# A decoder layer's MLP: first product by chunk pairs, w2's work in pieces, gate and residual at finished row blocks

## The chip, the cores and the metric

The kernel runs on one core of one Trainium2 chip. The metric is device time in microseconds (us) of one execution. The core has five engines with an instruction queue each: TensorE (PE, matmuls), VectorE (DVE), ScalarE (ACT), GpSimd (POOL) and SyncE (SP), which issues all DMA transfers between HBM and the on-chip memory (SBUF). Matmul results go to PSUM, which has eight banks of 128x512 float32. Each engine works its queue in order, and an instruction that waits holds up what stands behind it.

## The reference, cut to what matters

Sequence 2048, model width 1024, MLP width 4096, one layer, float32:

```python
    sh1, sc1, gt1, sh2, sc2, gt2 = split(silu(c) @ w_ada + b_ada)
    ...                                            # attention and retention give a and r
    y = concatenate([a, r]) @ w_out
    x = layer_norm(ALPHA * x + gt1 * y, ln1_g, ln1_b)
    h = x * (1.0 + sc2) + sh2
    f = square(relu(h @ w_ff1)) @ w_ff2
    x = layer_norm(ALPHA * x + gt2 * f, ln2_g, ln2_b)
```

The change lies in the last five lines.

## The kernel before, in words

**Products.** float32 precision is kept by splitting both operands of a product into a high and a low part: ACT copies to the high part (`split`, line 125), DVE or POOL subtracts to get the low part (line 128). `mm3` then runs three matmuls (lines 131 to 133), each 128x128 by 128x512. Both MLP products are tiled two by two, and each tile product is made with seven block products instead of eight (P1 to P7, added up in four accumulators X, Y, Z, W).

**The w_out stage** (lines 921 to 1010) goes over the 16 row blocks of 128 rows, last ones first. The weights are loaded in quarters, times the gate row gt1 (line 954), split, and kept in two pools: `wo0` for the left 512 columns, `wo1` for the right ones. Raw weights pass through `wor`, which has two buffers. For each row block, psY is the product; DVE adds the input residual (line 997) to get z; layer norm without gain follows on ACT. Then POOL makes x2 = z * (ALPHA ln1_g) + ALPHA ln1_b (lines 1003, 1004), and x2 goes to HBM (`ax2_d`): it is the residual of the last layer norm.

**The first MLP product** (`up`) goes over two halves of the rows (1024 each), and in a half over 16 chunks `c` of 256 MLP columns. A chunk has 84 matmuls of 512 columns: seven products of 12. The two w_ff1 tiles of a chunk are 512 KB loads (`w1r`), four in flight. Sums of weight blocks are made on POOL (DVE for the first four chunks, line 1074), then split into `w1h` and `w1l` (`w1p`, five buffers of each). `split_h` makes the seven h operands of a half (`hh`, `hl`), which stay until its end. Results are added on DVE out of PSUM, go through relu and square on ACT, and are stored to `g_d`. Chunks 0 and 1 run side by side, product by product; the others are written one after the other.

**w2's work** (`prep`) is done inside this stage, since the second product needs the same seven block combinations of w_ff2. A unit loads 1 MB (`w2r`, from the four `hraw` buffers), multiplies it by gt2 (line 1129, two DVE operations of 128x1024), and makes seven pieces: subtraction where needed, split into a tile `w2s`, store of 512 KB to `wt_d` (line 1137). `w2s` has two buffers, so a piece's split waits until the store of the piece two before it has landed. There are 16 units, eight in each half; `PREP` says after which chunk a unit is written down.

**The second MLP product** (`down`) goes over the two halves, and in a half over four steps `s` of 1024 MLP rows, seven products of 48 matmuls (each in two parts `q`). Its weights come back from `wt_d`, its activations `a4` from `g_d`. Results are added in SBUF (`acc`, one 128x1024 tile for a row block, line 1252). At s = 0 `acc` is loaded with the residual from `ax2_d` (`load_acc`), so all later work is addition. In the last step, P2 is taken ahead of P7 and P4: after it the first four row blocks of the half are complete, after P4 the other four. `finish` does the last layer norm: statistics on DVE (line 188), then either ACT, POOL times g2 (line 1199) and POOL or DVE plus b2 (line 1200), or, for t in FV4 of half 1, two `scalar_tensor_tensor` passes on DVE (lines 1191, 1194).

**What sets the order.** The program's text gives the dependencies; the order on each engine is laid out when the kernel is built, by a scheduler that goes by its own estimate of time (`schedule_with_timeline_sim`). Pools that are opened later may lie on the memory of pools that were closed; a tile then waits for what used the memory before. Instructions of text far apart may so stand next to each other in a queue.

## Time and profile before

| | us |
|---|---|
| median of three runs | 2646.72 (2644.70 to 2647.34) |
| the profiled execution: its time, its span | 2645.24, 2643.5 |
| last matmul of attention; first of w_out | 1080.23; 1082.26 |
| busy in the span: PE, DVE, ACT, POOL | 2457.8, 1809.5, 1188.1, 1126.6 |
| the last piece of w2 is issued | 1897.5 |

A row of the timeline gives start, length, engine, line, operation and operands (output <- inputs, with the partitions x elements of each), and in brackets how long the engine was idle before it and whom it waited for. PE's share is high everywhere, and since its matmuls overlap, a stretch is best judged by how many matmuls it holds: a stretch without losses has 443 in 100 us. The line numbers of the rows are those of the kernel before.

### The profile page before, as it was taken

What the parts mean: (1) busy time and instruction counts of PE and PEld (TensorE: products, weight loads), DVE (VectorE), ACT (ScalarE), POOL (GpSimd) and SP (SyncE); (2) the same over time, 40 slices, a digit from 0 to 9 for tenths busy, and PEclk for the clock granted to TensorE, in tenths of its full rate; (3) what the DMA queues carried; (4) which work ended last, traced back from release to release, by engine and by line L of the source; (5) the groups of instructions that cost most, each with busy time, mean ns of one, the idle gap of its engine ahead of it and who ended that gap; (6) DMA issues with size and microseconds to landing.
All of it is one profiled execution on the core that took longest, in us unless ns stands there. A gap on an engine that the chain in (4) does not pass through costs nothing.

```text
span 2643.5 us, 33756 instructions
## 1 busy us (share of the span) xinstructions
PE 2457.8 (93%) x11668; PEld 2028.1 (77%) x11668; DVE 1809.5 (68%) x2919; ACT 1188.1 (45%) x2317; POOL 1126.6 (43%) x1055
## 2 busy tenths in 40 slices
PE   6999999989999999899789999799999999999997
PEld 5887778877787878677577778677788888878885
DVE  8757675565767676766887755978645665776657
ACT  4653222246777777433455555455553111221111
POOL 4323545547978888577722223532220000330004
PEclk9999999988999999999889999899999999999998
DMA  9456341021112020655278863578838766776653
GB/s 327 146 196 224 108 133 50 31 73 32 48 37 61 20 62 13 219 183 192 104 263 268 280 229 107 174 255 278 293 123 349 271 245 256 295 301 244 225 191 127
DMA packets 194251, 464.69 MB, mean 176 GB/s; under 512 B 17560, under 2 KB 51736, under 8 KB 179744
## 3 DMA queue, kind: packets, MB, share of 16 engines
q1 hardware_dynamic: 194080, 462.54, 50.3%
q8 instruction: 92, 1.51, 0.2%
q14 instruction: 79, 0.65, 0.1%
HBM read 313.30 MB, written 149.17 MB: 175 GB/s over the span
## 4 chain that ended last, share of the span: by engine, by line
PE 54%; DVE 16%; DMA 13%; issue 6%; POOL 6%; ACT 5%; SPq 1%; DVEq 0%; ACTq 0%; POOLq 0%
DMA wt_d<-w2s 5%; PE d_W L131 4%; PE d_W L133 4%; PE d_W L132 4%; PE t L834 3%; DMA wad<-in_w_ada 2%; PE pj L133 2%; PE pj L132 2%; PE pj L131 2%; PE d_Z L132 2%; PE d_Z L133 2%; PE d_Z L131 2%; PE o L827 2%; PE o L825 2%; PE s L131 2%
## 5 line engine op out<-in xcount | busy, mean ns | idle before, releaser
L180 POOL TENSOR_SCALAR rs<-mv 128x1 f32<-128x1 f32 x32 | 16.0, 503 | 607.4 <-DVE mv L190 607.0
L128 DVE TENSOR_TENSOR w1l_P<-w,w1h_P 128x512 fp32r<-128x512 f32 x224 | 187.7, 844 | 69.4 <-ACT w1h_P L125 68.8
L806 ACT ACTIVATE p<-s,nm 128x512 f32<-128x512 f32 (+3 forms) x320 | 196.4, 627 | 41.8 <-DVE nm L803 38.3
L801 DVE TENSOR_REDUCE mx<-s 128x1 f32<-128x512 f32 (+3 forms) x288 | 175.0, 619 | 55.9 <-PE s L133 53.1
L1074 POOL TENSOR_TENSOR w<-w 128x512 f32<-128x512 f32 x56 | 81.7, 1463 | 286.7 <-DMA w<-in_w_ff 214.6
L125 ACT ACTIVATE w1h_P<-w 128x512 fp32r<-128x512 f32 x224 | 136.9, 622 | 108.2 <-PE u_Y L132 26.8
L850 POOL TENSOR_TENSOR tl<-tf,th 128x512 fp32r<-128x512 f32 x144 | 184.4, 1292 | 1.7
L834 PE MATMUL t<-ident,p 128*128 128x128 f32 x1088 | 164.3, 276 | 5.6 <-ACT tf L845 1.9
L834 PEld LDWEIGHTS t<-ident,p 128*128 128x128 f32 x1088 | 130.6, 142 | 30.8 <-ACT tf L845 6.1
L131 PE MATMUL pj<-wbh,hhb 128*128 128x512 f32 x384 | 151.3, 396 | 0.9 <-ACT wbh L125 0.5
L133 PE MATMUL pj<-wbh,hlb 128*128 128x512 f32 x384 | 152.1, 397 | 0.0
L132 PE MATMUL pj<-wbl,hhb 128*128 128x512 f32 x384 | 151.9, 396 | 0.2 <-DVE wbl L128 0.2
L131 PE MATMUL s<-kt,qt 96*128 96x512 f32 (+3 forms) x320 | 130.4, 408 | 11.5 <-ACT p L806 9.7
L1074 POOL TENSOR_TENSOR w<-w,w 128x512 f32<-128x512 f32 x56 | 81.8, 1461 | 133.8 <-DVE w1l_P L128 132.2
L128 DVE TENSOR_TENSOR w2s<-w2r,w2s 128x512 fp32r<-128x512 f32 x112 | 92.1, 825 | 66.8 <-ACT w2s L125 66.5
L125 ACT ACTIVATE w2s<-w2r 128x512 fp32r<-128x512 f32 x112 | 70.2, 628 | 146.0 <-DMA wt_d<-w2s 123.0
L827 PE MATMUL o<-tl,v 128*128 128x512 f32 (+2 forms) x320 | 123.3, 394 | 7.1 <-DVE tl L128 4.8
L825 PE MATMUL o<-th,v 128*128 128x512 f32 (+2 forms) x320 | 121.9, 385 | 5.6 <-DVE osum L861 4.5
L132 PE MATMUL s<-kt,qt 96*128 96x512 f32 (+3 forms) x320 | 120.4, 376 | 3.7 <-DVE kt L128 3.7
L133 PE MATMUL s<-kt,qt 96*128 96x512 f32 (+3 forms) x320 | 120.1, 376 | 0.0
L131 PE MATMUL u_W<-hh_P,w1h_P 128*128 128x512 f32 x256 | 102.6, 401 | 15.8 <-ACT hh_P L125 6.5
L133 PE MATMUL u_X<-hh_P,w1l_P 128*128 128x512 f32 x256 | 104.1, 408 | 12.4 <-DVE w1l_P L128 12.3
(372 smaller groups left out, 7850.6 us busy)
## 6 DMA issues: line engine op xcount, KB each, us to landing
wP<-wt_d SPq DMA_DIRECT2D x112, 1024.0 KB, 4.8
wt_d<-w2s SPq DMA_DIRECT2D x112, 512.0 KB, 4.9
w<-in_w_ff SPq DMA_DIRECT2D x64, 512.0 KB, 5.2
a<-g_d SPq DMA_DIRECT2D x32, 1024.0 KB, 6.3
g_d<-v SPq DMA_DIRECT2D x96, 256.0 KB, 4.2
wad<-in_w_ada SPq DMA_DIRECT2D x64, 256.0 KB, 2.9
w2r<-in_w_ff SPq DMA_DIRECT2D x16, 1024.0 KB, 7.7
x<-in_x SPq DMA_DIRECT2D x16, 512.0 KB, 8.2
```

The costliest lines, as they stand in the source:

```text
L125: A.activation(hi, x, AF.Copy)
L128: lo_eng.tensor_tensor(lo, x, hi.bitcast(F32), op=OP.subtract)
L131: T.matmul(ps, sh, mh, start=start, stop=False, skip_group_check=more)
L132: T.matmul(ps, sh, ml, start=False, stop=False, skip_group_check=more)
L133: T.matmul(ps, sl, mh, start=False, stop=stop, skip_group_check=more)
L801: V.tensor_reduce(mx[:, j:j + 1], ps[:, :n], op=OP.max, axis=AX.X)
L806: A.activation(pt[:, :m], b[:, :m], AF.Exp, bias=nm, accum_out=rs[:, qi, j:j + 1])
L825: T.matmul(po[:, cs], w, th[:, cs], start=(done == 0), stop=False)
L827: T.matmul(po[:, cs], w, tl[:, cs], start=False, stop=(done == nk))
L834: T.transpose(tp[:, qi * P:(qi + 1) * P], pts[h, 4 * qb + qi, kb // 4][1][:, kb % 4 * P:(kb % 4 + 1) * P], ident)
L850: (V if mode == "C" else G).tensor_tensor(tl[:, cs], tf[:, cs], th[:, cs].bitcast(F32), op=OP.subtract)
L1074: (V if half == 0 and c < W1V else G).tensor_tensor(src, *sub, op=op)
```

## The change

- **w_out stage.** The second multiplication row set (`ag1`, `ab1`) and x2 are gone; z itself is stored (`z_d`). The pools are opened in another order: `wo0` after `wo1`, `ax3` and `c3`.
- **First product.** All chunks run in pairs, product by product (P1 of both, P5 of both, ...), in the order P1, P5, P6, P7, P3, P4, P2. w_ff1 comes in quarters of 256 KB with two buffers for each quarter of each chunk of a pair. `split_h` hands out its seven operands one at a time, and those of half 1 are written into the last pair of half 0.
- **w2's work.** `prep` gives control back after every piece, and its 56 pieces of a half are written evenly between the products, from the seventh product step of the first pair on (a pair later in half 1). The multiplication by gt2 is gone.
- **Second product.** At s = 0 `acc` is no more loaded: the first addition to each quarter is an ACT copy out of PSUM. When a row block is complete, `residual` loads its z (two buffers, `ztp`) and makes x2 on POOL, and `gate` multiplies `acc` by gt2 and adds x2 on DVE. In the last product of half 1, gating is done ahead of the product, and the product's own results are gated one by one (tile y). `acc` of the first four row blocks has one buffer instead of two.
- **Buffers.** HSO and the pools of both products are opened in another order.

```diff
@@ w_out stage
     wor = pool(p3, "wor", 2)
-    wo0 = pool(p3, "wo0")
-    c3 = pool(p3, "c3")
     wo1 = pool(p3, "wo1")
     ax3 = pool(p3, "ax3", 2)
+    c3 = pool(p3, "c3")
+    wo0 = pool(p3, "wo0")
     x3 = pool(p3, "x3", 2)
-    c3b = pool(p3, "c3b")
...
-                    x2 = x3.tile([P, D], F32, tag="x2", name=f"x2_{tt}")
-                    G.tensor_tensor(x2, z, ag1, op=OP.mult)
-                    G.tensor_tensor(x2, x2, ab1, op=OP.add)
-                    Q.dma_start(ax2_d[tt], x2)
+                    Q.dma_start(z_d[tt], z)
@@ up, prep and their loop
-        for m in range(2):
-            t = w1r.tile([P, 2, 512], F32, tag="raw", name=f"w1_{half}_{c}_{m}")
-            Q.dma_start(t.rearrange("p j c -> p (j c)"), I["w_ff1"][2 * c + m].rearrange("p k c -> p (k c)"))
+        for m, j in ((0, 0), (1, 0), (1, 1), (0, 1)):
+            t = w1r.tile([P, 512], F32, tag=f"r{m}{j}", name=f"w1_{half}_{c}_{m}{j}")
+            Q.dma_start(t, I["w_ff1"][2 * c + m][:, 4 * j:4 * j + 4].rearrange("p k c -> p (k c)"))
...
-        for i in range(2):
-            V.tensor_tensor(b[:, i], b[:, i], gt2, op=OP.mult)
...
             Q.dma_start(wt_d[s][x][k // 2][:, :, k % 2], t.bitcast(F32))
+            yield
...
+        slots = [i for i in range(7 * NCH) if half or i < 7 * NCH - 8]
+        slots = slots[14:] if half else slots[12:]
+        nxt = split_h(1, Hn) if half == 0 else None
+        for c in range(0, NCH, 2):
+            pair = [up(half, x, H) for x in (c, c + 1)]
+            for x in range(7):
+                for y in range(2):
+                    next(pair[y], None)
+                    i = 7 * c + 2 * x + y
+                    if i in slots:
+                        while count < min(want, -(-(slots.index(i) + 1) * want // len(slots))):
+                            next(todo, None)
+                            count += 1
+                if nxt is not None and c == NCH - 2:
+                    next(nxt, None)
@@ second product
+    def residual(half, t):
+        zt = ztp.tile([P, D], F32, tag="zt", name=f"zt{half}_{t}")
+        with tc.issue_after(wdma[-1]):
+            Q.dma_start(zt, z_d[4 * border[2 * half + t // 4] + t % 4])
+        G.tensor_tensor(zt, zt, ag1, op=OP.mult)
+        G.tensor_tensor(zt, zt, ab1, op=OP.add)
+        return zt
+
+    def gate(f, zt):
+        V.tensor_tensor(f, f, gt2, op=OP.mult)
+        V.tensor_tensor(f, f, zt, op=OP.add)
+
     def finish(half, t):
         f = acc[t]
+        if half == 0 or t < 4:
+            gate(f, residual(half, t))
...
                 ops = [parts(q) for q in range(2)]
                 for tp in range(4):
+                    gate(acc[4 + tp], residual(half, 4 + tp))
+                for tp in range(4):
                     for k in range(4):
                         mm(tp, k, *ops[k // 2])
+                    y = ztp.tile([P, D], F32, tag="zt", name=f"y{tp}")[:, 0:512]
+                    V.tensor_tensor(y, ps[ch, tp], gt2[:, 0:512], op=OP.mult)
+                    V.tensor_tensor(acc[4 + tp][:, 0:512], acc[4 + tp][:, 0:512], y, op=OP.add)
+                return
...
-                        load_acc(half, 4 * i + tp)
+                        acc[4 * i + tp] = acs[4 * i + tp].tile([P, D], F32, tag="c", name=f"acc{half}_{4 * i + tp}")
                     c = acc[4 * i + tp][:, 512 * j:512 * j + 512]
-                    V.tensor_tensor(c, c, ps[ch, tp], op=OP.add)
+                    if s == 0 and name in ("P1", "P5", "P6", "P4"):
+                        A.activation(c, ps[ch, tp], AF.Copy)
+                    else:
+                        V.tensor_tensor(c, c, ps[ch, tp], op=OP.add)
```

How the change moves instructions is shown at three places. In a row stand line, operation, output <- inputs, and size; names carry the half and chunk (or step), and a running number that differs from build to build.

ACT in half 0 of the first product, before, from chunk 4's P7 on (w1h is a split of a w_ff1 block, w2s one of a w2 piece, u, v and r are results):

```order
L125 ACTIVATE w1h0_4_P7_15626<-w1_0_4_0_15565 128x512
L125 ACTIVATE w2s2_2_15726<-w2r2_15712 128x512
L1090 ACTIVATE v0_3_15555<-v0_3_15555 128x512
L125 ACTIVATE w1h0_4_P2_15643<-w1_0_4_0_15565 128x512
L1091 ACTIVATE v0_3_15555<-v0_3_15555 128x512
L125 ACTIVATE w1h0_4_P3_15662<-w1_0_4_1_15567 128x512
L1100 ACTIVATE u0_4_15622<-u0_4_X_15573 128x512
L125 ACTIVATE w2s2_3_15730<-w2r2_15712 128x512
L1090 ACTIVATE v0_3_15560<-v0_3_15560 128x512
L1091 ACTIVATE v0_3_15560<-v0_3_15560 128x512
L125 ACTIVATE w1h0_4_P4_15686<-w1_0_4_1_15567 128x512
L125 ACTIVATE w2s2_4_15734<-w2r2_15712 128x512
```

ACT in the same half after the change, at the pair of chunks 4 and 5:

```order
L126 ACTIVATE w1h0_4_P1_15508<-w1_0_4_00_15496 128x512
L126 ACTIVATE w2s2_6_15921<-w2r2_15682 128x512
L1090 ACTIVATE v0_3_15431<-v0_3_15431 128x512
L1091 ACTIVATE v0_3_15431<-v0_3_15431 128x512
L126 ACTIVATE w1h0_5_P1_15540<-w1_0_5_00_15528 128x512
L1090 ACTIVATE v0_2_15457<-v0_2_15457 128x512
L126 ACTIVATE w2s3_0_15964<-w2r3_15962 128x512
L1091 ACTIVATE v0_2_15457<-v0_2_15457 128x512
L126 ACTIVATE w1h0_4_P5_15557<-w1_0_4_10_15498 128x512
L126 ACTIVATE w2s3_1_16006<-w2r3_15962 128x512
L1090 ACTIVATE v0_3_15487<-v0_3_15487 128x512
L1091 ACTIVATE v0_3_15487<-v0_3_15487 128x512
```

In both, w2's pieces stand one at a time between the splits of the products. Over 14 products (two chunks), ACT's queue in half 0 has 3, 10, 11, 13, 12 and 7 pieces before, and 9, 10, 13, 12 and 12 now; in half 1 it has 4, 7, 12, 13, 13 and 7 before, and 8, 12, 13, 14 and 9 now.

DVE in the last step of half 0's second product, before, from the last addition of P2's result (X3) to the additions of P7's result (W0 and W1; gP4l is the low part of P4's operand, BN_STATS and BN_AGGR belong to the statistics):

```order
L1252 TENSOR_TENSOR acc0_3_20401<-acc0_3_20401,d0_3_X3_22047 128x512
L188 BN_STATS st_22140<-acc0_2_20398 128x6
L188 BN_STATS st_22154<-acc0_3_20401 128x6
L128 TENSOR_TENSOR gP4l0_3_0_22235<-a4_0_3_11_21766,gP4h0_3_0_22234 128x1024
...
L188 BN_STATS st_22154<-acc0_3_20401 128x6
...
L199 TENSOR_SCALAR nm_22132<-mv_22129,rs_22131 128x1
L128 TENSOR_TENSOR gP4l0_3_1_22265<-a4_0_3_11_21766,gP4h0_3_1_22264 128x1024
L199 TENSOR_SCALAR nm_22146<-mv_22143,rs_22145 128x1
L199 TENSOR_SCALAR nm_22160<-mv_22157,rs_22159 128x1
L1252 TENSOR_TENSOR acc0_4_20470<-acc0_4_20470,d0_3_W0_21772 128x512
L1252 TENSOR_TENSOR acc0_5_20473<-acc0_5_20473,d0_3_W1_21773 128x512
```

DVE there after the change:

```order
L1213 TENSOR_TENSOR acc0_1_20431<-acc0_1_20431,gt2_20352 128x1024
L1297 TENSOR_TENSOR acc0_3_20435<-acc0_3_20435,d0_3_X3_22083 128x512
L1213 TENSOR_TENSOR acc0_2_20433<-acc0_2_20433,gt2_20352 128x1024
L129 TENSOR_TENSOR gP4l0_3_0_22295<-a4_0_3_11_21802,gP4h0_3_0_22294 128x1024
L1214 TENSOR_TENSOR acc0_1_20431<-acc0_1_20431,zt0_1_22168 128x1024
L1213 TENSOR_TENSOR acc0_3_20435<-acc0_3_20435,gt2_20352 128x1024
L1214 TENSOR_TENSOR acc0_2_20433<-acc0_2_20433,zt0_2_22188 128x1024
L189 BN_STATS st_22174<-acc0_1_20431 128x6 x2
L129 TENSOR_TENSOR gP4l0_3_1_22325<-a4_0_3_11_21802,gP4h0_3_1_22324 128x1024
L189 BN_STATS st_22194<-acc0_2_20433 128x6 x2
L1297 TENSOR_TENSOR acc0_4_20503<-acc0_4_20503,d0_3_W0_21808 128x512
```

The multiplications by gt2 (L1213) and the additions of the residual (L1214, the residual tile is zt) now stand between P2's additions and the splits for P4 and ahead of P7's additions.

POOL in the tail, before, from the first row block that half 1 finishes (the sequence L180, L181 makes the reciprocal deviation, three rows of it left out):

```order
L1199 TENSOR_TENSOR acc1_0_22424<-acc1_0_22424,g2_20316 128x1024
L1200 TENSOR_TENSOR acc1_0_22424<-acc1_0_22424,b2_20317 128x1024
L180 TENSOR_SCALAR rs_24163<-mv_24161 128x1
...
L181 TENSOR_TENSOR rs4_24191<-rs4_24191,mhalf_115 128x1
L1199 TENSOR_TENSOR acc1_1_22427<-acc1_1_22427,g2_20316 128x1024
L1199 TENSOR_TENSOR acc1_2_22430<-acc1_2_22430,g2_20316 128x1024
L1200 TENSOR_TENSOR acc1_2_22430<-acc1_2_22430,b2_20317 128x1024
```

POOL in the tail after the change, from the second residual on:

```order
L1209 TENSOR_TENSOR zt1_1_24240<-zt1_1_24240,ab1_20354 128x1024
...
L1208 TENSOR_TENSOR zt1_2_24260<-zt1_2_24260,ag1_20353 128x1024
L1235 TENSOR_TENSOR acc1_0_22508<-acc1_0_22508,g2_20355 128x1024
L1209 TENSOR_TENSOR zt1_2_24260<-zt1_2_24260,ab1_20354 128x1024
L1236 TENSOR_TENSOR acc1_0_22508<-acc1_0_22508,b2_20356 128x1024
L1208 TENSOR_TENSOR zt1_3_24280<-zt1_3_24280,ag1_20353 128x1024
L1209 TENSOR_TENSOR zt1_3_24280<-zt1_3_24280,ab1_20354 128x1024
L1208 TENSOR_TENSOR zt1_4_24376<-zt1_4_24376,ag1_20353 128x1024
L181 TENSOR_SCALAR rs_24251<-mv_24249 128x1
L181 TENSOR_SCALAR rs_24271<-mv_24269 128x1
```

The tail's multiplications by g2 (now L1235) and additions of b2 (L1236) now alternate with the residual's two operations (L1208, L1209), which are done eight times in a half.

## Rows read from the trace of the kernel before

**Rows 1.** The page: busy us, share of the span, instructions, by engine.

```profile
PE 2457.8 (93%) x11668; PEld 2028.1 (77%) x11668; DVE 1809.5 (68%) x2919; ACT 1188.1 (45%) x2317; POOL 1126.6 (43%) x1055
```

**Rows 2.** Stretches: start:end us, length, busy us (instructions) by engine, granted clock, DMA share, GB/s.

```profile
1285.00:1345.00 60.00, 37.57 (x138) 29.12 (x138) 51.94 (x46) 26.68 (x34) 36.33 (x16) 0.72 0.37 133
1345.00:1561.00 216.00, 200.14 (x836) 159.81 (x835) 164.26 (x225) 119.87 (x214) 48.91 (x33) 0.97 0.83 274
1645.00:1705.00 60.00, 46.37 (x171) 35.47 (x170) 59.82 (x44) 28.08 (x43) 42.47 (x18) 0.86 0.42 136
1741.00:1897.00 156.00, 145.30 (x611) 115.44 (x611) 122.98 (x165) 92.57 (x165) 42.78 (x28) 0.98 0.80 270
...
2100.00:2200.00 100.00, 100.00 (x443) 82.82 (x442) 57.78 (x66) 20.17 (x19) 0.00 (x0) 1.00 0.69 251
2278.00:2344.00 66.00, 59.69 (x254) 48.33 (x253) 60.15 (x67) 19.98 (x18) 43.82 (x28) 0.97 0.84 320
2591.00:2643.50 52.50, 32.68 (x133) 26.20 (x131) 43.71 (x59) 8.17 (x7) 27.47 (x23) 0.84 0.29 112
```

**Rows 3.** Timeline, POOL, w_out weights times the gate: start, length, group, idle before.

```profile
1077.51 2.52 POOL L954 TENSOR_TENSOR wo<-wo,gt 128x512 f32<-128x512 f32 x2
1087.22 1.42 POOL L954 TENSOR_TENSOR wo<-wo,gt 128x512 f32<-128x512 f32 x1 [7.18 <-DMA wo<-in_w_out]
1091.47 1.87 POOL L954 TENSOR_TENSOR wo<-wo,gt 128x512 f32<-128x512 f32 x1 [2.83 <-DMA wo<-in_w_out]
```

**Rows 4.** Waits of PE, 1282 to 1345 us: who waited for whom, total, times, longest.

```profile
PE u_Y L132 <- DVE hl_P L128: 10.0, 2, 7.3
PE u_W L131 <- ACT hh_P L125: 6.5, 1, 6.5
PE u_Z L132 <- DVE hl_P L128: 3.8, 1, 3.8
```

**Rows 5.** Pieces of w2, half 0 (1330 to 1570): operations, then idle before them.

```profile
L125 ACT ACTIVATE w2s<-w2r x56: 614/632/635, 1334.7 to 1553.5; 128x512 fp32r<-128x512 f32 x56
L128 DVE TENSOR_TENSOR w2s<-w2r,w2s x56: 676/691/1815, 1336.3 to 1554.2; 128x512 fp32r<-128x512 f32 x56
L1137 SPq DMA_DIRECT2D wt_d<-w2s x56: 512/525/1177, 1337.0 to 1554.9; - x56
...
  DMA wt_d<-w2s: 68.8, 33
```

**Rows 6.** The same, half 1 (1685 to 1900 us).

```profile
L1137 SPq DMA_DIRECT2D wt_d<-w2s x56: 512/524/1293, 1691.7 to 1897.5; - x56
```

**Rows 7.** The page, DMA issues: count, KB each, median us to landing.

```profile
wt_d<-w2s SPq DMA_DIRECT2D x112, 512.0 KB, 4.9
...
w2r<-in_w_ff SPq DMA_DIRECT2D x16, 1024.0 KB, 7.7
```

**Rows 8.** The multiplications by gt2 in the pieces' way (line 1129).

```profile
L1129 DVE TENSOR_TENSOR w2r<-w2r,gt x32: 1211/1218/3423, 1333.4 to 1815.6; 128x1024 f32<-128x1024 f32 x32
```

**Rows 9.** Timeline of the tail: DVE and then POOL, at 2591 to 2614 us.

```profile
2591.20 0.69 DVE L1252 TENSOR_TENSOR acc<-acc,d_X 128x512 f32<-128x512 f32 x1 [0.47 <-PE d_X L133]
...
2608.51 5.50 DVE L1194 SCALAR_TENSOR_TENSOR acc<-acc,rs,b 128x512 f32<-128x512 f32 x2
...
2595.89 2.40 POOL L1199 TENSOR_TENSOR acc<-acc,g 128x1024 f32<-128x1024 f32 x1 [1.61 <-ACT acc L1198]
...
2607.70 5.75 POOL L1199 TENSOR_TENSOR acc<-acc,g 128x1024 f32<-128x1024 f32 x2
```

**Rows 10.** Groups in the tail, 2591 to 2643.5: count | busy, mean ns | idle before.

```profile
L1191 DVE SCALAR_TENSOR_TENSOR acc<-acc,mv,g 128x512 f32<-128x512 f32 x8 | 5.6, 744 | 0.0
...
L128 DVE TENSOR_TENSOR gP4l<-a,gP4h 128x1024 fp32r<-128x1024 f32 x2 | 2.4, 1210 | 0.0
```

**Rows 11.** Groups where half 0 ends and half 1 begins (2278 to 2345).

```profile
L1199 POOL TENSOR_TENSOR acc<-acc,g 128x1024 f32<-128x1024 f32 x8 | 22.8, 2866 | 5.0 <-ACT acc L1198 5.0
L1200 POOL TENSOR_TENSOR acc<-acc,b 128x1024 f32<-128x1024 f32 x4 | 13.2, 3310 | 0.2
```

120 lines of the change are left out of this document (64 added, 56 removed).

## The prediction

> **What bounds the kernel now.** I read the page first: PE is busy 93% of the span [rows 1], so a gain can only come from stretches where PE holds fewer matmuls than it could, and a loss from new such stretches. The table of stretches measures them. From 2100 to 2200 us PE issues 443 matmuls in 100 us at granted clock 1.00, 0.2257 us each; a stretch's loss is its length less its matmuls times that. By this, with [rows 2]: 60 - 138 x 0.2257 = 28.9 us are lost around the start of the first MLP product; 216 - 836 x 0.2257 = 27.3 where half 0 shares its time with w2's work; 60 - 171 x 0.2257 = 21.4 at the change of halves; 156 - 611 x 0.2257 = 18.1 with w2's work of half 1; 66 - 254 x 0.2257 = 8.7 where the second product changes halves. The tail runs from the addition of P2's result at 2591.20 [rows 9] to the end at 2643.5: 52.3 us, of which PE needs 133 x 0.2257 = 30. All that the change can win lies in the first four, about 96 us; what it adds lies in the last two.
>
> Two mechanisms decide. One is the **ring of two buffers** of w2's pieces: ACT was idle 68.8 us, 33 times, until a store had landed [rows 5], and the 56 pieces of a half leave every (1554.9 - 1337.0) / 55 = 3.96 us in half 0 and every (1897.5 - 1691.7) / 55 = 3.74 us in half 1 [rows 5, 6]. The other is that **DVE and POOL take turns** when both work from SBUF: two scalar_tensor_tensor halves of DVE, 0.74 us each by the mean of the undisturbed pass [rows 10], last 5.50 us beside two POOL multiplications, and these last 5.75 instead of twice the 2.40 of one alone [rows 9]. 1.5 + 4.8 = 6.3 is the time that both took together, from 2607.70 to 2608.51 + 5.50 = 2614.01. So I add DVE's operations with two SBUF inputs to POOL's, where both are queued; additions out of PSUM and statistics are left out of that sum.
>
> **The change, part by part.**
>
> *A. w_out's left weights.* Their last six quarters go through the two-buffer pool in three rounds, now at 1077.51, 1087.22 and 1091.47 [rows 3], so two of the three run while attention ends or psY has just begun. In the new order all three stand behind the right half's. The rounds are 4.25 us apart when nothing else is in the way and 9.7 at most. Three from 1091.47 end at 1104.3 to 1120.6; PE needs them after the 96 matmuls of the first two row blocks, 1082.26 + 96 x 0.2257 = 1103.9. Cost 0 to 17; I take **+9**, halfway. The 32 POOL operations of x2 that leave this stage are worth nothing by themselves; they count in B.
>
> *B. Start of the first product.* PE waits 10.0 + 6.5 + 3.8 = 20.3 us for the h operands [rows 4], because their work queues behind POOL's x2. In the new order four of the seven are split before psY ends, so these waits go. What is late next: on DVE the first subtraction of w2's first unit stands ahead of the first w1 split, and its 1 MB load takes 7.7 us [rows 7]. -20.3 + 7.7: **-13**, bounds -20 (the load is early) and -4.
>
> *C. w2's work.* The text now deals pieces evenly, but the scheduler had interleaved them before: the ACT rows of both kernels show one piece between two splits, and the counts for 14 products (10 to 13 before, 12 to 14 now) are higher now. Before, the pieces of half 0 lie between the 8th and 78th product in ACT's queue (70 products), now between the 4th and 67th (63); in half 1 it is 69 before and 60 now. A product is 12 x 0.2257 = 2.71 us, so PE would pass those places in 170.6 and 162.5 us. What it waits for is 55 times the ring's pace. The gt2 multiplications leave DVE's queue, 32 x 1.218 us [rows 8] over 112 pieces: 0.35 us each. So 3.61 and 3.39: 198.6 - 170.6 + 186.5 - 162.5 = 52 lost, against 27.3 + 18.1 = 45.4 now: **+7**. If the pace stays, 217.9 - 170.6 + 205.8 - 162.5 = 90.6: +45. If it falls below a product's 2.7 us, the whole 45 is won: -45. These are far apart; I take the value nearest the row, since 0.63 (ACT) + 0.69 (DVE) + 0.53 (SP) [rows 5] + 4.9 for landing [rows 7] is 6.75 for two pieces in flight, 3.4 a piece, with nothing between.
>
> The Trainium skill ("DMA: Bandwidth & Descriptors", "Anatomy of one DMA") fits 2.0 us plus the bytes over 436 GB/s for a DMA of another issuing path. For 512 KB that is an estimate of 3.2 us, so the ring could turn in 2.5 and C would be -45, the sum near 0. The landing row says 4.9 where the engines move some 270 GB/s, so the page's figure doesn't hold here.
>
> *D. Change of halves.* The seven operands of half 1 are the same operations, but given out through the last pair of half 0 and the first of half 1. The loss was 21.4; I take **-10**, half of it, since each operand still frees one of half 0's only after that half's last product that uses it; bounds -18 and 0.
>
> *E. The rest.* Twice as many w1 loads of half the size (64 more DMAs on SP), 16 loads of z for 16 of x2, five rows for all partitions in step 1 of half 0: hidden, unless a quarter's buffer is freed late. The 16 first additions become ACT copies, with ACT busy 20 of 66 us there [rows 2]. **+1**, 0 to +5.
>
> *F. Second product, change of halves.* Eight row blocks get two POOL operations and two DVE operations each (2.40 and 1.2 us, [rows 9, 10]) = 57.6 us of turn-taking. Before, POOL had 8 + 4 operations here [rows 11], which already last 2.87 and 3.31. In the new DVE queue 40 operations of 128x1024 with two SBUF inputs stand between P2's first addition and the last split for P7 of half 1's first step; POOL must do 20 by then (the first two residuals are earlier). 40 x 1.2 + 20 x 2.40 = 96 us. PE passes there in six and a half products, 6.5 x 48 x 0.2257 = 70.4. That is 25.6 lost if they pack without a gap, less the 8.7 lost already: +17. Above, nothing of the new work finds a gap: 57.6 less the four early POOL operations and the old loss, 57.6 - 9.6 - 8.7 = +39. I take **+24**, nearer to the lower end, since DVE and POOL still left gaps before (60.2 and 43.8 busy of 66 us, [rows 2]). Queued behind the gates on DVE are P7's additions, for which P4 waits, and P4's own splits.
>
> *G. Tail.* After P2's first addition, DVE has 16 gate operations, three splits and one addition of b2 (20 x 1.2 = 24), 16 scalar_tensor_tensor halves (11.8) and four additions of y (4 x 0.69 = 2.8): 38.6. POOL has 19 operations: 12 of residuals, 7 as before: 45.6. Together 84.2, against 52.3 for the whole tail now, of which the same kinds make 4.8 + 11.8 + 7 x 2.40 = 33.4. +32 if they pack, +45 with the present gaps (52.3 - 33.4 = 18.9) largely kept; **+34**. The residual's two buffers make this worse: each load waits for the gate of two blocks before.
>
> Sum: 9 - 13 + 7 - 10 + 1 + 24 + 34 = **+52**. The profiled execution took 2645.24, so 2697; it lies 1.5 below the median of the runs shown, so I say **2698**.
>
> **Rivals.**
> 1. *The first product recovers.* The ring keeps up (C -45), start and change of halves give their best (B -20, D -18, A 0, E 0), F and G as above: -83 + 58 = -25, 2620. For it: the gt2 multiplications gone, pairs give each split twice the time. Against: landing takes 4.9 us whatever the order. It decides below 2.7 us a piece. Chance 0.20.
> 2. *Residual and gate are hidden.* POOL is idle from 2100 to 2200 and DVE 42% [rows 2]; if z's loads and POOL's work came early, F would be 0 and G about +4, the sum -2: 2643. Against: two buffers, and the order that puts the rest behind P2's end. Chance 0.11.
> 3. *The ring keeps its old pace.* Then packing pieces into fewer products costs +45 in C, the sum is +90: 2735. Decided by whether the gt2 rows were in the ring's way at all. Chance 0.13.
>
> **How the numbers follow.** The forecast has 0.56. The range is 2632 to 2738: low enough for rival 2 and the better half of C's bounds, high enough for rival 3; most of rival 1 (0.14) and 0.06 above are left out. 0.2%, about 5 us, is what can be told from no change here. Faster: 0.20 + 0.06 of rival 2 = 0.26; same: 0.04 of rival 2 + 0.02 = 0.06; slower: 0.68.
>
> **What would show it.** After the change, pieces should leave every 3.4 to 3.6 us in both halves, with ACT still idle for landing stores; PE should show a loss of some 30 us after the last P2 of half 0's second product, with DVE rows of 128x1024 at 2 to 3.5 us beside POOL's; the tail from P2's first addition should last some 86 us. Wrong are: A, if psY's third row block starts before 1108; C, if PE shows no waits for w1h or w1l between the first pair and the last piece; F and G, if POOL's residual operations run before P2's end.

## The result, and the profile after the change

The changed kernel took 2690.65 us (median; 2689.74 to 2691.44), the kernel before 2645.71 (2642.19 to 2647.34) beside it: a ratio of 1.0172, 95% interval 1.0154 to 1.0189. The profiled execution has a span of 2689.6 us, 46.1 more than before. The direction, the size (2698 foretold) and the mechanism of the two terms that carry it (F and G) were right. A, the first product (B, C, D) and E missed by -6.8, -9.2 and +7.1 us, G by +7.5 and F by +0.6, and attention, which no term names, came out 5.0 shorter: these misses largely cancel, to -5.8 in sum, and that is luck.

The page of the kernel after, busy us by engine, to be held against [rows 1]: PE, DVE and POOL have as much work as before (PE has the same 11668 matmuls), in a longer span. What changed is where the work lies.

```profile
PE 2447.0 (91%) x11668; PEld 2028.9 (75%) x11668; DVE 1815.3 (67%) x2891; ACT 1209.6 (45%) x2349; POOL 1148.1 (43%) x1055
```

Cutting the span at events that both traces have gives the stages, in us. They run up to: the last matmul of attention; the last psY; the middle and the last matmul of the first product; the first of the second product ("gap"); DVE's first addition of P2's result in half 0's last step (this stretch is "second product, half 0", below also "down 0"); PE's first P2 matmul in half 1's first step ("change"); DVE's first addition of P2's result in half 1's last step; the end of the span ("tail").

| | before | after | difference | foretold |
|---|---|---|---|---|
| up to attention's end | 1080.2 | 1075.2 | -5.0 | |
| w_out | 208.2 | 210.4 | +2.2 | A +9 |
| first product, half 0 | 371.5 | 354.0 | -17.5 | B, C, D together |
| first product, half 1 | 342.0 | 334.3 | -7.7 | -16 |
| gap | 0.7 | 8.8 | +8.1 | E +1 |
| second product, half 0 | 275.1 | 276.8 | +1.7 | F +24, |
| change | 92.9 | 115.8 | +22.9 | these two |
| half 1 | 220.5 | 220.5 | 0 | |
| tail | 52.3 | 93.8 | +41.5 | G +34 |

The first product's half 0 is counted from the last psY on, so it holds the 16.0 us up to the first u matmul (1.0 before).

The table of stretches after the change, with the columns of [rows 2]:

```profile
1285.00:1345.00 60.00, 40.03 (x173) 32.12 (x172) 51.53 (x65) 36.14 (x53) 22.38 (x11) 0.83 0.70 242
1295.00:1510.00 215.00, 193.99 (x821) 156.07 (x821) 171.85 (x228) 128.17 (x220) 53.32 (x32) 0.95 0.85 290
1639.00:1836.00 197.00, 180.53 (x761) 147.18 (x760) 161.69 (x196) 116.93 (x206) 65.81 (x40) 0.96 0.82 281
2278.00:2362.00 84.00, 62.32 (x233) 48.08 (x232) 79.52 (x70) 24.61 (x29) 68.22 (x34) 0.88 0.54 198
2595.80:2689.60 93.80, 32.93 (x133) 26.35 (x131) 85.25 (x81) 7.99 (x7) 63.32 (x35) 0.67 0.26 96
```

The first row now loses 60 - 173 x 0.2257 = 21.0 us (28.9 before). The fourth, where the second product changes halves, loses 84 - 233 x 0.2257 = 31.4 (8.7 before), and DVE is busy for 79.5 of its 84 us. In the tail, DVE is busy 85.3 of 93.8 us and PE does the same 133 matmuls as before.

Why, the timeline of the tail shows (start, length, group), DVE first, then POOL:

```profile
2609.13 3.42 DVE L129 TENSOR_TENSOR gP4l<-a,gP4h 128x1024 fp32r<-128x1024 f32 x1
2612.47 3.42 DVE L1214 TENSOR_TENSOR acc<-acc,zt 128x1024 f32<-128x1024 f32 x1
2615.82 1.21 DVE L1213 TENSOR_TENSOR acc<-acc,gt 128x1024 f32<-128x1024 f32 x1
...
2620.41 1.27 DVE L189 BATCH_NORM_STATS2 st<-acc 128x6 f32<-128x512 f32 x2
2621.61 0.66 DVE L1297 TENSOR_TENSOR acc<-acc,d_W 128x512 f32<-128x512 f32 x1
...
2604.75 3.37 POOL L1235 TENSOR_TENSOR acc<-acc,g 128x1024 f32<-128x1024 f32 x1
2608.08 3.38 POOL L1209 TENSOR_TENSOR zt<-zt,ab 128x1024 f32<-128x1024 f32 x1
2611.43 3.38 POOL L1236 TENSOR_TENSOR acc<-acc,b 128x1024 f32<-128x1024 f32 x1
2620.36 2.35 POOL L1208 TENSOR_TENSOR zt<-zt,ag 128x1024 f32<-128x1024 f32 x1 [5.54 <-DMA zt<-z_d]
```

POOL's row that starts at 2608.08 ends at 2611.46; DVE's split, at hand since 2609.13, ends at 2612.55, 1.1 us later, about what it takes alone (1.21). POOL's next row then ends at 2614.81, 2.3 us after that, and DVE's next at 2615.89, again 1.1 later: strict turns, each waiting for the whole of the other. At 2620 DVE takes statistics and adds out of PSUM beside POOL, and neither is held (2.35 and 1.27). The Trainium skill ("SBUF — State Buffer", "SBUF: two separate sides") says just this: a DVE operation with two SBUF inputs and a POOL operation that reads SBUF share a pair of ports, which whichever starts first holds for its whole instruction. The trace agrees: an operation of 1.21 us lasts 3.42 beside one of 2.40.

### The profile page after: what moved, and what is told of

Read it like the earlier page. It is cut to its first block, busy times and chain, and to the rows that moved or that the text cites. A ratio compares the mean times of both kernels' runs of the same rounds, so it can differ in the third digit from the quotient of the medians.

```text
span 2689.6 us, 33970 instructions
## 1 busy us (share of the span) xinstructions
PE 2447.0 (91%) x11668; PEld 2028.9 (75%) x11668; DVE 1815.3 (67%) x2891; ACT 1209.6 (45%) x2349; POOL 1148.1 (43%) x1055
## 4 chain that ended last, share of the span: by engine, by line
PE 62%; DVE 16%; DMA 10%; issue 5%; ACT 4%; POOL 2%; SPq 0%; DVEq 0%; ACTq 0%; POOLq 0%
DMA wt_d<-w2s 4%; PE d_W L132 4%; PE d_W L133 4%; PE d_W L134 4%; PE t L835 3%; DMA wad<-in_w_ada 2%; PE o L826 2%; PE o L828 2%; PE d_Z L134 2%; PE d_Z L133 2%; PE pj L134 2%; PE d_Z L132 2%; PE pj L132 2%; PE pj L133 2%; PE s L132 2%
## 5 line engine op out<-in xcount | busy, mean ns | idle before, releaser
L1076 POOL TENSOR_TENSOR w<-w,w 128x512 f32<-128x512 f32 x112 | 167.7, 1503 | 377.7 <-DVE w1l_P L129 234.2
L129 DVE TENSOR_TENSOR w1l_P<-w,w1h_P 128x512 fp32r<-128x512 f32 x224 | 194.6, 872 | 65.7 <-ACT w1h_P L126 64.4
L807 ACT ACTIVATE p<-s,nm 128x512 f32<-128x512 f32 (+3 forms) x320 | 196.6, 627 | 39.7 <-DVE nm L804 36.2
L1208 POOL TENSOR_TENSOR zt<-zt,ag 128x1024 f32<-128x1024 f32 x16 | 44.1, 2762 | 355.6 <-DMA zt<-z_d 355.6
L126 ACT ACTIVATE w1h_P<-w 128x512 fp32r<-128x512 f32 x224 | 138.1, 622 | 97.4 <-PE u_Y L133 25.2
L129 DVE TENSOR_TENSOR w2s<-w2r,w2s 128x512 fp32r<-128x512 f32 x112 | 98.0, 876 | 57.7 <-ACT w2s L126 57.2
L132 PE MATMUL u_Z<-hh_P,w1h_P 128*128 128x512 f32 x256 | 104.9, 410 | 28.4 <-DVE v L1105 28.4
L132 PE MATMUL psY<-wo_h,mh 128*128 128x512 f32 x256 | 101.1, 400 | 10.8 <-ACT wo_h L126 10.3
L129 DVE TENSOR_TENSOR tl<-t,th 128x512 fp32r<-128x512 f32 (+3 forms) x176 | 92.7, 539 | 26.9 <-ACT th L126 25.7
```

Of the source, the lines that this page charges most:

```text
L126: A.activation(hi, x, AF.Copy)
L129: lo_eng.tensor_tensor(lo, x, hi.bitcast(F32), op=OP.subtract)
L132: T.matmul(ps, sh, mh, start=start, stop=False, skip_group_check=more)
L807: A.activation(pt[:, :m], b[:, :m], AF.Exp, bias=nm, accum_out=rs[:, qi, j:j + 1])
L1076: (V if half == 0 and c < W1V else G).tensor_tensor(src, *sub, op=op)
```

## The experiments

The ratios are against the kernel before, timed beside each. The stages of all profiled executions, in us (names as above; "up 0" and "up 1" are the halves of the first product):

| run | w_out | up 0 | up 1 | gap | down 0 | change | half 1 | tail | span |
|---|---|---|---|---|---|---|---|---|---|
| before | 208.2 | 371.5 | 342.0 | 0.7 | 275.1 | 92.9 | 220.5 | 52.3 | 2643.5 |
| after | 210.4 | 354.0 | 334.3 | 8.8 | 276.8 | 115.8 | 220.5 | 93.8 | 2689.6 |
| x2_early | 224.0 | 360.6 | 333.1 | 16.1 | 276.9 | 99.3 | 220.5 | 73.2 | 2673.0 |
| res_dve | 209.8 | 350.0 | 330.8 | 8.6 | 276.9 | 103.0 | 220.5 | 83.1 | 2658.1 |
| ztp4 | 210.5 | 353.3 | 331.7 | 8.4 | 278.3 | 115.8 | 220.5 | 89.1 | 2681.8 |
| gt2_prep | 210.5 | 356.7 | 339.5 | 8.7 | 283.9 | 109.3 | 220.5 | 76.9 | 2683.3 |
| up_only | 207.5 | 373.4 | 344.3 | 17.2 | 277.8 | 94.5 | 220.5 | 51.5 | 2661.8 |
| old_up | 209.1 | 359.3 | 339.7 | 11.7 | 277.2 | 112.4 | 220.5 | 94.0 | 2698.3 |
| wo0_first | 196.6 | 362.2 | 331.0 | 8.8 | 276.8 | 112.0 | 220.5 | 93.8 | 2677.6 |
| mid | 210.3 | 359.0 | 338.7 | 8.7 | 296.6 | 87.2 | 234.0 | 51.5 | 2659.8 |
| mid_old | 211.2 | 363.5 | 340.9 | 12.1 | 290.3 | 87.1 | 234.1 | 51.5 | 2663.6 |
| spread | 210.6 | 358.1 | 342.0 | 8.8 | 281.0 | 87.2 | 220.5 | 52.1 | 2634.5 |
| spread_wl | 210.8 | 360.0 | 338.1 | 2.2 | 281.9 | 87.2 | 220.5 | 52.4 | 2631.5 |
| spread_all | 196.4 | 361.6 | 340.1 | 2.8 | 283.2 | 87.2 | 220.5 | 51.5 | 2620.5 |

One caution: res_dve and ztp4 have the first product's text unchanged, and it takes 680.8 and 685.0 us in them against 688.3 after the change. The order is laid out anew in every build, so a difference below some 8 us in the first product can't be put down to an edit.

### What the finishing stretches cost

**res_dve**: the residual's two operations on DVE instead of POOL.

```diff
-        G.tensor_tensor(zt, zt, ag1, op=OP.mult)
-        G.tensor_tensor(zt, zt, ab1, op=OP.add)
+        V.tensor_tensor(zt, zt, ag1, op=OP.mult)
+        V.tensor_tensor(zt, zt, ab1, op=OP.add)
```

> The changed kernel with the residual's two operations on DVE instead of POOL, nothing else. Theory 1 (turn-taking): a POOL operation of 2.40 us is replaced by one of 1.2 in the same shared time, so the tail's sum falls from 84 to 84 - 12 x 1.2 = 70 and the tail from 93.8 to about 80; the change of halves gains about 10; 2660 to 2675. Rival (DVE is the bound by itself, POOL's work was free): 16 more DVE operations in each half cost 14 us in the tail and 10 to 14 at the change of halves, 2700 or more.

Measured 2662.94 us (2659.87 to 2664.32), ratio 1.0073 (1.0052 to 1.0094): 28 us faster than the change, by giving DVE, the busier of the two engines, 32 more operations. The finishing stretches make 23.5 of it (tail -10.7, change of halves -12.8, as foretold); the first product's -7.5 is no more than a new order moves. Groups of its tail, from 2590 us on (count | busy, mean ns):

```profile
L1214 DVE TENSOR_TENSOR acc<-acc,zt 128x1024 f32<-128x1024 f32 x7 | 12.5, 1801 | 0.0
...
L1208 DVE TENSOR_TENSOR zt<-zt,ag 128x1024 f32<-128x1024 f32 x5 | 5.9, 1203 | 0.6 <-DMA zt<-z_d 0.6
```

An operation that holds the ports for 2.40 us on POOL holds them for 1.20 on DVE. Had the two engines worked side by side, this edit would have made it slower. That turns are taken is shown.

**x2_early**: x2 is made in the w_out stage again and stored, the gate stays at the end.

```diff
+                    G.tensor_tensor(x2, z, xg1, op=OP.mult)
+                    G.tensor_tensor(x2, x2, xb1, op=OP.add)
-                    Q.dma_start(z_d[tt], z)
+                    Q.dma_start(z_d[tt], x2)
...
     def residual(half, t):
-        G.tensor_tensor(zt, zt, ag1, op=OP.mult)
-        G.tensor_tensor(zt, zt, ab1, op=OP.add)
```

> The changed kernel, but x2 is made by POOL in the w_out stage again and loaded ready; the gate on DVE stays. 24 POOL operations of 128x1024 leave the two finishing stretches, 32 come back in w_out. Theory 1 (turn-taking): the tail from P2's first addition has 38.6 + 7 x 2.40 = 55 us of turn-taking instead of 84, so 93.8 falls to some 70 to 75; the other change of halves loses some 12 instead of 33; up to 10 come back at the start of the first product. 2650 to 2665. Rival (the finishing stretches are long because a gate stands in DVE's queue ahead of other work, POOL doesn't matter): tail within 8 us of 93.8, 2680 or more.

Measured 2678.91 us (2673.69 to 2683.89), ratio 1.0135 (1.0108 to 1.0162), just short of the rival's 2680, yet the tail fell to 73.2 as the theory had it. Against the change, tail and change of halves give back 20.6 + 16.5 = 37 us, w_out takes 13.6, and the first product 5.4, which is within what a new order moves. The gap takes 7.3, in which PE waits for the second product's first weights (15.7 us of the 16.1). So x2's removal from the early stages was worth some 14 to 19 us there, and its new place cost 37; the total lies 14 us above the expected range, since more came back early than the 10 us allowed for, and the gap grew.

**gt2_prep**: gt2 is multiplied into w2 again; `gate` only adds the residual.

```diff
+        for i in range(2):
+            V.tensor_tensor(b[:, i], b[:, i], gt2, op=OP.mult)
...
-        V.tensor_tensor(f, f, gt2, op=OP.mult)
         V.tensor_tensor(f, f, zt, op=OP.add)
```

> The changed kernel with gt2 multiplied into w2 again, and no multiplication in the gate (the residual stays where the change puts it; three and one result buffers instead of four and two for gt2's memory). Theory 1 (a ring of w2 pieces that DVE's queue slows, and turn-taking at the finishing stretches): the second half of the first product takes some 10 us more (344 instead of 334), the tail 10 to 15 less, the change of halves 8 to 12 less: 2672 to 2684. Rival (gt2's multiplications cost the same wherever they stand, 1.2 us each on DVE): 2688 to 2694.

Measured 2685.27 us (2679.89 to 2688.84), ratio 1.0149 (1.0131 to 1.0168), between the two expectations. The stages tell more: tail -16.9, change -6.5, against down 0 +7.1 and the first product +7.9. The last is no larger than what a new order alone moves. What gt2 costs the ring of w2's pieces can be read, though, from the stores of the two halves (times in ns, then first and last start):

```profile
L1140 SPq DMA_DIRECT2D wt_d<-w2s x56: 512/519/613, 1311.3 to 1525.9; - x56
...
L1140 SPq DMA_DIRECT2D wt_d<-w2s x56: 512/519/798, 1656.8 to 1855.0; - x56
```

Pieces leave every 3.90 and 3.60 us, where the change, without gt2, has 3.64 and 3.41; stores land alike (4.0 and 3.9 us by the pages). So gt2's rows were in the ring's way, by 0.26 and 0.19 us a piece where the prediction took 0.35. The ring is 25 us longer in sum, the first product only 7.9: in half 0 PE passes 70 products beside the pieces, not 65.

**ztp4**: four buffers for the residual instead of two, paid for with one of the five weight buffers.

```diff
-WLB = 5
+WLB = 4
-    ztp = pool(p4b, "ztp", 2)
+    ztp = pool(p4b, "ztp", 4)
```

> The changed kernel with four buffers for z instead of two (and four instead of five for w2's weights, to make room). Theory 1 (turn-taking sets the finishing stretches): four more POOL operations come ahead of P2's end in each half, 4 x 2.40 = 9.6 us less in each: 2670 to 2682. Rival (the two buffers set them: every load of z waits for a gate two row blocks before): the tail falls by 20 us or more and the change of halves as well, 2650 or less.

Measured 2687.21 us (2683.57 to 2688.09), ratio 1.0164 (1.0142 to 1.0185), above what either expected. The tail is 4.7 shorter, the change of halves is not: this missed the turn-taking expectation too, which took four POOL operations out of each finishing stretch. In the tail the waits for z's loads go, but DVE's multiplications by gt2 then take 2458 ns (group of its tail) where they took 2158:

```profile
L1213 DVE TENSOR_TENSOR acc<-acc,gt 128x1024 f32<-128x1024 f32 x8 | 19.4, 2458 | 0.0
```

What POOL no longer waits for, it takes from DVE. The two buffers were a small part of the tail; what the weight buffer given up for them costs, no run tells.

### What the first product and the start are worth

**up_only**: the kernel before, with the change's first product and pieces (gt2 still in w2, x2 still in w_out, second product as before).

```diff
-        for c in range(NCH):
...
-            if c in PREP[half]:
-                prep(8 * half + PREP[half].index(c))
+        for c in range(0, NCH, 2):
+            pair = [up(half, x, H) for x in (c, c + 1)]
+            for x in range(7):
+                for y in range(2):
+                    next(pair[y], None)
...
-HSO = 6, 5, 4, "u", "w", 0, 1, 2, 3
+HSO = 6, 4, "u", 5, 3, 2, "s", "o", 0, 1, "w"
```

> The kernel before with the first product alone as changed (pairs, w_ff1 in quarters, w2's work in pieces, its pool order); w_out, x2, the multiplication by gt2 in w2's work and the second product are as before. One and three result buffers instead of two and four, since gt2 takes their memory. Theory 1 (turn-taking of DVE and POOL in the second product costs all of the loss, the first product gains): 2620 to 2641, from 2645.7 by the gains read at the start, half 0 and the change of halves (8 to 26 us). Rival (the pairs cost as much as they bring, since P3 now waits for DVE's addition out of Z): 2646 or more.

Measured 2662.27 us (2660.86 to 2664.15), ratio 1.0071 (1.0046 to 1.0096): the rival. With x2 and gt2 left in place, pairs and evenly dealt pieces gain nothing in the first product (717.7 us against 713.5), and the gap ahead of the second is 17.2: in its wait list there PE waits for the first weights alone.

```profile
PE d_W L132 <- DMA wP<-wt_d: 16.9, 1, 16.9
```

**old_up**: the reverse, the change with the first product, its loads and its buffers as before (w2 without gt2).

```diff
-        for c in range(0, NCH, 2):
-            pair = [up(half, x, H) for x in (c, c + 1)]
+        for c in range(NCH):
...
+            if c in PREP[half]:
+                prep(8 * half + PREP[half].index(c))
...
-        for m, j in ((0, 0), (1, 0), (1, 1), (0, 1)):
+        for m in range(2):
```

> The changed kernel with the first product and w2's work written as before (chunks one after the other, units whole, w_ff1 in 512 KB, the old pool order there), but without the multiplication by gt2; w_out, z, residual and gate stay changed. Theory 1 (pairs and pieces bring nothing by themselves; the first product got shorter because x2 left its start and gt2 left DVE's queue): 2680 to 2700, with the first product within 10 us of the changed kernel's. Rival (pairs and pieces make the gain): the first product is 20 us longer or more, 2708 or above.

Measured 2703.67 us (2700.11 to 2708.91), ratio 1.0227 (1.0208 to 1.0246), between theory and rival. Its first product takes 699.0 us against 688.3 after the change and 713.5 before: without x2 and gt2 the old form already gains 14.5, and pairs add some 11, little above what order alone moves.

**wo0_first**: the change with w_out's pools opened in the order of before.

```diff
+    wo0 = pool(p3, "wo0")
+    c3 = pool(p3, "c3")
     wo1 = pool(p3, "wo1")
     ax3 = pool(p3, "ax3", 2)
-    c3 = pool(p3, "c3")
-    wo0 = pool(p3, "wo0")
```

> The changed kernel with the pools of w_out in the order of the kernel before (wo0 ahead of wo1), nothing else. Theory of the prediction's part A: psY starts about 7 us earlier after attention, and PE has no waits of 10.3 and 8.7 us for wo_h and wo_l; 9 us less in all, 2676 to 2685. Rival (the late start is given back inside the stage, since the later row blocks then find z and the axl operands ready): within 4 us of 2690.

Measured 2680.46 us (2677.39 to 2684.68), ratio 1.0139 (1.0112 to 1.0165): as the theory of A has it. In the change, three rounds of POOL's multiplications by the gate start well into the stage (timeline of the kernel after, POOL), and PE waits for the split weights (its wait list, w_out):

```profile
1094.99 3.31 POOL L954 TENSOR_TENSOR wo<-wo,gt 128x512 f32<-128x512 f32 x2 [3.52 <-DVE axl L987]
1105.90 2.56 POOL L954 TENSOR_TENSOR wo<-wo,gt 128x512 f32<-128x512 f32 x2 [7.61 <-DMA wo<-in_w_out]
1111.79 2.55 POOL L954 TENSOR_TENSOR wo<-wo,gt 128x512 f32<-128x512 f32 x2 [3.33 <-DMA wo<-in_w_out]
```

```profile
PE psY L132 <- ACT wo_h L126: 10.3, 2, 8.7
PE psY L133 <- DVE wo_l L129: 8.7, 2, 6.6
```

With the old order the last round is at 1088.77, these waits shrink to 0.6 us, and the stage takes 196.6. That is 11.6 less than before the change, with x2's operations gone. The first product is 4.9 longer than after the change, which order alone could do. Counted up to the first u matmul, it is 209.6 us from attention's end, against 226.4 after the change and 209.3 before: in both changed kernels PE waits for the last row blocks' z ahead of the first u.

### Where residual and gate could go instead

**mid**: gt2 in w2, and all eight residuals of a half added together after its step s = 1; nothing is left for the finishing stretches.

```diff
+            if s == 1:
+                for t in range(8):
+                    V.tensor_tensor(acc[t], acc[t], residual(half, t), op=OP.add)
...
-            gate(f, residual(half, t))
```

> The changed kernel with gt2 multiplied into w2 again, and with the residual made by POOL and added by DVE after the second of the four steps of each half, where POOL is idle, instead of where row blocks are finished; acc still begins with an ACT copy. Theory 1 (the loss is turn-taking at the finishing stretches alone): both finishing stretches as long as in the kernel before (tail 52, the step after the change of halves 70), the first product 10 longer than in the changed kernel: 2632 to 2645. Rival (32 POOL and 16 DVE operations more in the second product cost their time wherever they are): 2660 or more.

Measured 2662.04 us (2660.51 to 2664.67), ratio 1.0064 (1.0049 to 1.0079): the rival. Tail and change of halves are back, even better than before, but the place of the eight residuals now loses 20 and 13.5 us. PE's wait list there, and DVE's timeline at half 0:

```profile
PE d_Z L132 <- DVE acc L1290: 9.3, 1, 9.3
```

```profile
2139.14 3.36 DVE L1325 TENSOR_TENSOR acc<-acc,zt 128x1024 f32<-128x1024 f32 x1
...
2144.76 1.21 DVE L129 TENSOR_TENSOR gP1l<-a,gP1h 128x1024 fp32r<-128x1024 f32 x1
...
2148.17 3.40 DVE L129 TENSOR_TENSOR gP1l<-a,gP1h 128x1024 fp32r<-128x1024 f32 x1
```

Even in a stretch where POOL had been idle, 16 POOL operations in a lump make a DVE split take 3.40 us instead of 1.21, and PE waits for DVE. Rival 2's hiding place exists, but not for all at once.

**mid_old**: the same with the first product as before (the diff of old_up).

> The same as the last kernel, with the first product and w2's work as before the change (gt2 in the same place). Theory 1 (pairs and pieces bring nothing; the end of the first product got 8 to 16 us worse by the other order of the pools): 2625 to 2640, not above the kernel with pairs. Rival (pairs and pieces shorten the first product): 12 us or more above the kernel with pairs.

Measured 2665.65 us (2663.65 to 2668.87), ratio 1.0078 (1.0063 to 1.0093). This missed the expectation twice: by mid's own loss in the middle steps, and because it lies 3.6 above mid and not below. Its first product takes 704.4 against 697.7; 6.7 us is within what order alone moves, so with gt2 in w2's work pairs are worth a few us at most.

**spread**: as mid, but one residual after each of the first four products of steps 1 and 2.

```diff
         prod(0, "P1", "W", True, a11, [], (0, 0))
+        spread(half, s, 0)
         prod(1, "P5", "Z", True, a21, [(a21, a21, a22, plus)], (1, 1))
+        spread(half, s, 1)
...
+    def spread(half, s, i):
+        if s in (1, 2):
+            t = 4 * (s - 1) + i
+            V.tensor_tensor(acc[t], acc[t], residual(half, t), op=OP.add)
```

> The kernel with gt2 in w2's work and the residual in the middle of the half (mid), but one row block's residual behind each of the first four products of the second and the third step, instead of eight together. There DVE had waited for POOL's residual with the additions out of Z queued behind it (PE waited 9.3 us in either half, and the stretch from the last P2 of one half to that of the next grew by 14 to 21). Theory 1 (a matter of place: POOL's and DVE's work fits where DVE is 42% idle): those stretches come back to within 5 us of the kernel before, 2630 to 2642. Rival (they take their time wherever they are): above 2655.

Measured 2635.62 us (2631.76 to 2640.52), ratio 0.9967 (0.9954 to 0.9980): as expected, and 0.3% faster than the kernel before. Half 1 is at 220.5 again, as if no residual were there.

**spread_wl**: spread, with the second product's pools opened so that the weights' buffers (`wl`) take the memory that comes free first.

```diff
+    wl = pool(p4b, "wl", WLB)
+    raws = {i: pool(p4b, f"raw{i}") for i in (0, 2, 3)}
+    gp = pool(p4b, "gp", GB)
+    raws[1] = pool(p4b, "raw1")
...
     c4 = pool(p4b, "c4")
-    gp = pool(p4b, "gp", GB)
-    wl = pool(p4b, "wl", WLB)
```

> The last kernel with the pools of the second product in another order: w2's weights and three of the activation buffers first, on memory that the first product leaves early. Theory (the 8.7 us between the two products are the first weights' late load, and the load is late because of the buffers' memory): the gap falls below 3 us, 5 to 8 less than the last kernel. Rival (the load is late because it stands behind the stores of results in SP's queue, or gP1h behind the last results on ACT): within 3 us of the last kernel.

Measured 2631.63 us (2627.20 to 2633.32), ratio 0.9952 (0.9933 to 0.9971). The gap falls from 8.8 to 2.2 us as expected; the total's interval overlaps spread's. The edit moves the activations' pools (`raw`, `gp`) as well as the weights', and in spread's wait list PE's 8.5 us ahead of the second product end with ACT's gP1h, a split of the first activations. So the order of the pools is what counts; which pool, no run tells.

**spread_all**: spread_wl, with w_out's pools as in wo0_first.

> The kernel spread_wl with w_out's pools opened in the order of before (wo0, c3, wo1, ax3). With the changed kernel, this edit took the gap ahead of the first psY from 9.0 to 2.0 us and o_end to psY_end from 210.4 to 196.6, and 11 us came back later in half 0 of the first product, since w2's work there sets the pace. Theory: the stage's part is a true cost, of which some stays won here too: 2622 to 2629 us, and the w_out stage 10 us or more shorter than in spread_wl. Rival (all of it is given back because the first product is held by w2's work): 2630 us or more with the same shorter stage. Above 2636 the new order was worth something that I have missed.

Measured 2623.06 us (2622.31 to 2623.66), ratio 0.9925 (0.9911 to 0.9938): as the theory had it, and about 20 us faster than the kernel before. (The 11 us that the expectation has coming back in half 0 are 8.2 by the table above.) The table of stretches of spread_all, over the steps with residuals, and two lines of the view of the residual's tiles (duration min/median/max in ns):

```profile
2054.00:2206.00 152.00, 152.00 (x672) 125.86 (x671) 117.34 (x104) 31.92 (x32) 46.24 (x16) 1.00 0.76 282
```

```profile
L1214 POOL TENSOR_TENSOR zt<-zt,ag x16: 2389/2421/3478, 2056.4 to 2475.4; 128x1024 f32<-128x1024 f32 x16
L1215 POOL TENSOR_TENSOR zt<-zt,ab x16: 2397/3262/3280, 2058.9 to 2478.3; 128x1024 f32<-128x1024 f32 x16
```

PE issues 672 matmuls in 152.0 us, 672 x 0.2257 = 151.7: no loss at all, with 16 POOL operations in the stretch. POOL is still held by DVE (3.26 us), but with one row block to a product, turn-taking fits into the gaps. (That down 0 is 8 us longer here than before the change lies at its start: 2.4 + 2.4 + 1.8 us of PE's waits there are for splits of the first two products' activations, ahead of any residual.)

## Why the prediction was right, and where it was not

**A, w_out: +2.2 for +9.** The mechanism is there: psY's third row block starts at 1121.8 in the timeline (1109.8 before), far behind the 1108 that would have refuted it, and wo0_first prices the new order at 210.4 - 196.6 = 13.8 us, inside the 0 to 17; x2_early prices it the same way, 15.8 us above the kernel before with x2 in both. What failed is the sentence that x2's 32 POOL operations are worth nothing in this stage: wo0_first, which has the old order and no x2, is 11.6 us shorter than before. POOL and DVE took turns there too: DVE's 16 additions to the input residual (`axl`, line 987) have a median of 3.41 us before and 1.22 in wo0_first.

**B, C, D, first product: -25.2 for -16.** *B.* The waits for the h operands are gone, as foretold. What is late in their place is not w2's first load: PE's transposes wait for z of the last row blocks (wait list of the kernel after, 1284 to 1345).

```profile
PE psT L965 <- ACT z L1001: 12.8, 2, 8.6
```

The start gave 28.9 - 21.0 = 8 of its 13.

*C.* The ring's pace was met. Pieces leave every 3.64 us in half 0 and 3.41 in half 1, for 3.61 and 3.39 foretold, and the chain of waits inside the stage, from 1400 to 1460, runs through it (start, length, what; of its 25 longest pieces):

```profile
1402.27 0.69 DVE w2s L129
1402.97 3.94 DMA wt_d<-w2s
1406.99 0.64 ACT w2s L126
...
1408.94 8.29 DMA w2r<-in_w_ff
...
1453.27 0.64 ACT w2s L126
1453.93 0.69 DVE w2s L129
1455.74 0.68 DVE v L1105
```

The figure was met with some luck. Stores land in 3.9 us now, so the sum that I held it against would give (0.63 + 0.69 + 0.52 + 3.9) / 2 = 2.9; the chain shows what else stands between the pieces, such as 8.29 us for the load of a unit. In gt2_prep stores land 0.9 us earlier than before the change, and its pace is only 0.06 and 0.14 us faster: the earlier landing brought little. Of the gain of 0.32 and 0.33 us, 0.26 and 0.19 are gt2's, for 0.35. C's loss fits as well: (215 - 821 x 0.2257) less the 6.6 us up to the first u is 23.1, and 197 - 761 x 0.2257 is 25.2, 48 in all for 52.

The step that failed is that B, C and D were summed as if they stood one after the other. Half 0's first piece is now stored at 1306.3, 4.7 us behind the first u matmul (47.5 before), and half 1's at 1648.3, 8.7 behind the middle of the stage (31.7 before). So most of the loss at the change of halves lies inside C's second figure, and a 7.2 us wait of the start inside its first, and both are paid once. D by itself: the last pair of half 0 and the first of half 1 (336 matmuls) take 97.7 us before, from 1618.4, and 91.1 after, from 1596.1, so -6.6 for -10.

Where PE waits, the list for 1306 to 1836 shows:

```profile
PE u_Z L132 <- DVE v L1105: 28.4, 7, 7.2
PE u_Y L134 <- DVE w1l_P L129: 3.4, 1, 3.4
PE u_Z L134 <- DVE w1l_P L129: 2.2, 1, 2.2
```

The test that I set (waits for w1h and w1l) is met by some 7 us only; the bulk sits at another place. P3 adds to the accumulator Z, and its first matmul may not run before DVE has read Z for v. In five of the seven waits (17.7 us) v stands in DVE's queue behind a piece of w2, as in the last two rows of the chain (two short operations lie between them). The longest, 7.2 us at 1322.8, and one of 3.6 at 1624.3 stand behind work for the h operands that took turns with POOL, such as:

```profile
1317.99 3.36 DVE L129 TENSOR_TENSOR hl_P<-h,hh_P 128x1024 fp32r<-128x1024 f32 x1
```

Whoever looks for a ring's cost must look at everything that shares the ring's queue, not just at the splits. That the ring holds PE is read from these waits; no run gave w2s a third buffer to show it by an edit.

**What the change wins here.** up_only and old_up together say that the gain of 25 comes with x2 and gt2 leaving (14.5 with the old form), with some 11 from pairs given that, little above what order alone moves; pairs alone bring none.

**E, the rest: +8.1 for +1.** The first weights of the second product are issued when the first is as good as over (1973.37, against 1988.82 for a first matmul at 2002.7 before), and `wl` is opened late, on memory that pools of the first product held (that this is why they are late is argued, not shown). PE waits for them (wait list of the kernel after, 1974 to 2000):

```profile
PE d_W L132 <- DMA wP<-wt_d: 8.4, 1, 8.4
```

The new order of the second product's buffers stands in the change, and the prediction priced it nowhere. spread_wl shows that the order of the pools makes the gap: 8.8 against 2.2 us.

**F, change of halves: +22.9 for +24.** Counting DVE's two-input operations and POOL's in one queue gave this almost exactly, with some luck. PE's waits there, for DVE's splits above all, grew from 6.3 us (2278 to 2344 before) to 21.7 (2278 to 2362 after); their two largest entries after, and the whole list before:

```profile
PE d_Z L134 <- DVE gP5l L129: 6.7, 2, 4.7
PE d_W L134 <- DVE gP6l L129: 5.7, 2, 5.5
```

```profile
PE d_Z L133 <- DVE gP5l L128: 3.8, 1, 3.8
PE d_W L133 <- DVE gP6l L128: 2.5, 2, 2.1
```

That is 15.4 of the 22.9 us; the rest is about what the lower clock behind these waits can cost (at most 10 us, last section), and the sum had no term for it. **G, tail: +41.5 for +34**, within its 32 to 45. The term was undersized by taking the stretch as nearly packed (84.2 of 86): the groups of the tail show the gaps, POOL idle until z's loads land and until DVE has a variance.

```profile
L1214 DVE TENSOR_TENSOR acc<-acc,zt 128x1024 f32<-128x1024 f32 x8 | 18.2, 2276 | 4.6 <-POOL zt L1209 4.5
L1213 DVE TENSOR_TENSOR acc<-acc,gt 128x1024 f32<-128x1024 f32 x8 | 17.1, 2158 | 0.0
...
L1208 POOL TENSOR_TENSOR zt<-zt,ag 128x1024 f32<-128x1024 f32 x6 | 16.0, 2672 | 6.3 <-DMA zt<-z_d 6.3
...
L181 POOL TENSOR_SCALAR rs<-mv 128x1 f32<-128x1 f32 x8 | 4.3, 548 | 19.0 <-DVE mv L191 19.0
```

res_dve shows the mechanism: halving the time that the residual holds the ports took 10.7 us from the tail (14 foretold) and 12.8 from the change of halves (10).

**The rivals.** Rival 1 fell because the ring's floor held; the first product gave 25 us, not 83. Rival 2 describes what the kernel would need and doesn't do: most of the residual's operations stand behind P2's end, and only spread, which moves them, reaches it. Rival 3 fell with the pace of 3.64 us.

Not settled is the start: attention ends 1069 to 1079 us into the span in all changed builds, 1080.2 before, though no edit touches it. I have no run that tells what moves it.
